# A hybrid attention and RWKV-7 layer in float32: later steps for transfers, norms and transposes handed on, one product tile for two heads

## The chip, the cores and the metric

The kernel runs on one core of a Trainium2 chip. The metric is the device time of one execution in microseconds; the median of several runs is given with the lowest and the highest.

## The reference

One encoder layer on x of 1024 positions by 1024 channels, all in float32. `proj` has 26 column tiles of 128: 12 for the attention's q, k and v, 14 for the recurrent part. The scan below runs forward and backward over all positions.

```python
h = _rms_norm(x, ln1_g)
proj = h @ w_in
q, k, v, u = proj[..., :512], proj[..., 512:1024], proj[..., 1024:1536], proj[..., 1536:]
attn = _dilated_window_attention(q, k, v, q_norm_g, k_norm_g)   # 8 heads of 64, 3 windows, ALiBi
rwkv = _rwkv7_bidirectional(u, ...)                             # 8 heads of 64
x = x + concatenate([attn, rwkv]) @ w_out
h = _rms_norm(x, ln2_g)
x = x + square(relu(h @ w_up)) @ w_down

def _dilated_window_attention(q, k, v, q_g, k_g):
    q = _rms_norm(q, q_g) * HEAD_DIM ** -0.5                    # norm over each head's 64 channels
    k = _rms_norm(k, k_g)
    ...
def step(state, inp):                                           # of _wkv7_scan
    r_t, w_t, k_t, v_t, kk_t, a_t = inp
    s_kk = einsum('bhvk,bhk->bhv', state, kk_t)
    state = state * w_t - s_kk * (kk_t * a_t) + v_t * k_t
    return state, einsum('bhvk,bhk->bhv', state, r_t)
```

## The kernel before

**Dense projections.** Each of the 26 column tiles is computed transposed (128 channels by 1024 positions) in two halves of 512 positions. Operands are split in a rounded and a remainder part, so one product is three matmuls (`mm3`, L105 to L107), and a half tile takes 8 × 3 = 24 of them. `proj` yields after every six. `dense()` runs the tiles in the order of a list: the recurrent tiles for head pair 0 first, then those for pairs 1, 2 and 3, then q, k and v tiles. At the end of each half tile `evac` takes the result out of PSUM. For q and k (`qk_tile`) it scales into `qc` (L322), squares it (`qsq`, L324), sums the squares by head on TensorE and inverts (`head_inv`, product L124, `rn` L127 and L128), widens that to 512 columns and takes the root (`rx`, L133), turns it on TensorE (L136), multiplies (`qc`, L326), splits into `qhi` and `qlo`, and stores both in DRAM (`qh_dr`/`kh_dr`, `ql_dr`/`kl_dr`, L332 and L333). For v it transposes and stores. `qsq`, `qhi` and the value tile `vn` share one buffer (tag `qt`).

**The recurrent part.** It is computed in chunks of 64 positions. For each head pair p (0 to 3) and each half of the positions, `per_half` computes the normed key, the transposed values (`VT`, stored to `vt_dr`, L432) and the decay (`om`, L443). `unit_a` then forms for each direction `al` and `bk`, their products for both heads (`psg`, L496, masked into `G`, L501), stores them to DRAM (`gd` and `rec_dr`), and turns `bk` (`psb`, L508, copied to `BK`, L512, stored by ScalarE's queue, L513). `bonus` is a small product. When both halves of a direction are ready, `pair_b` goes on the list `back`: it loads the diagonal 16 × 16 blocks as `MP` (L524), clears `Tt` (L527 and L528, POOL), inverts the blocks by a chain of 15 pairs of small VectorE instructions (`stmp`, L534, and L536), stores the result (`td`, L543) and loads it in another shape (`t16`, `t16t`, with `Ab`, L550 and L553). `unit_c` extends it to 64 × 64 by four products (`psd`, L564) and stores `TF`.

**What sets the order.** All these are Python generators, advanced by hand. `drive` runs one recurrent generator; after each yield it advances the first entry of `back` by 0.6 steps on average (`behind`) and the dense projections by 0.7 steps (`next(filler)`), a step being six matmuls or one `yield` between tiles. `until` runs projections until a tile that is needed is there. After the last head pair a loop empties `back`, four dense steps to each of its steps. The framework then schedules the instructions of each engine from this program order, and an instruction waits by semaphores for what it needs. DMAs are issued by SP, and a few by ScalarE (ACT) and POOL.

**After it.** `mixers` runs 16 steps of the scan (products `psc`, L870), two directions in each, with what is left of the projections and then the attention's pieces between them. Then come the output projection and the MLP.

## Time and profile before

| | |
|---|---|
| median of three runs | 1788.32 us (1781.92 to 1796.67) |
| the profiled execution | 1784.77 us |
| its span | 1783.0 us |
| mean granted TensorE clock | 0.949 |
| recurrent preparation, of the span | 151 to 510 us |
| the loop that empties `back` | 510 to 604 us |
| first scan steps with the last projections | 604 to 680 us |
| scan and attention | 680 to 990 us |
| output projection and MLP | 990 to 1783 us |

Engines are PE (TensorE), DVE (VectorE), ACT (ScalarE), POOL (GpSimd) and SP. PEld is TensorE's weight load. L12 is a line of the kernel before. A row of a timeline has start, duration, engine, line, operation, output<-inputs with their shapes, and in brackets the idle time before it with what ended it. A row of waits has the waiting engine and line, what it waited for, the total, the number of times and the longest. PEclk is the granted clock, as a share of full speed.

### The profile page before, as it was taken

Reading aid. Unit: us, or ns where it says so; the run is one execution under the profiler, and the core shown is the slowest. Engines: PE = TensorE matmul, PEld = TensorE weight load, DVE = VectorE, ACT = ScalarE, POOL = GpSimd, SP = SyncE. Lnnn points to the kernel's source line nnn. Section 1 sums busy time; section 2 is a strip of 40 time slices with the busy share of each in tenths; the row PEclk is TensorE's granted clock in tenths of the full one; section 3 lists DMA queues with packets and bytes.
Section 4 is the critical chain, followed back from the end, with each engine's and each line's share of the span. In section 5 each row is a group of like instructions: output and inputs, shape, how many; then the busy total and the mean of one; then the engine's idle time right before and its main releaser. Section 6 shows DMA issues by size and latency. Waiting matters only on the chain. (4 is left out here: it accounts for less than half of the span.)

```text
span 1783.0 us, 29922 instructions
## 1 busy us (share of the span) xinstructions
PE 1649.5 (93%) x11912; PEld 1365.7 (77%) x11912; DVE 861.9 (48%) x1754; ACT 543.5 (30%) x990; POOL 294.2 (16%) x322
## 2 busy tenths in 40 slices
PE   7999978979869997989998999999999999999999
PEld 6777767767757776877786887888888888888887
DVE  6655658757545424565775667332332233223321
ACT  5534334443412213535464234211121112112210
POOL 3022112222200000121223115200120012001200
PEclk9999989879879999988998999999999999999999
DMA  6155788878875599997973411111111111111121
GB/s 221 45 142 125 158 160 174 177 176 176 193 173 135 179 223 202 274 272 210 248 198 108 149 48 54 49 53 48 51 50 47 48 48 48 48 48 54 47 96 53
DMA packets 336923, 223.11 MB, mean 125 GB/s; under 512 B 238320, under 2 KB 289408, under 8 KB 332688
## 3 DMA queue, kind: packets, MB, share of 16 engines
q1 hardware_dynamic: 305520, 195.82, 42.7%
q10 hardware_dynamic: 27680, 15.38, 3.2%
q0 software_dynamic: 3584, 10.00, 2.5%
q8 instruction: 94, 1.54, 0.4%
q14 instruction: 45, 0.37, 0.1%
HBM read 150.22 MB, written 70.91 MB: 124 GB/s over the span
## 5 line engine op out<-in xcount | busy, mean ns | idle before, releaser
L101 ACT CAST w3h<-w3raw 128x512 fp32r<-128x512 f32 (+1 forms) x152 | 90.9, 600 | 397.0 <-PE ps L106 387.3
L106 PE MATMUL ps<-h2l,w3h 128*128 128x512 f32 x512 | 199.2, 389 | 1.1 <-DVE h2l L1045 1.1
L105 PE MATMUL ps<-h2h,w3h 128*128 128x512 f32 x512 | 199.3, 390 | 0.7 <-DVE x L1023 0.7
L107 PE MATMUL ps<-h2h,w3l 128*128 128x512 f32 x512 | 199.2, 389 | 0.0
L1089 POOL TENSOR_TENSOR relu<-relu 128x512 f32<-128x512 f32 x64 | 76.8, 1201 | 530.1 <-DVE relu L1088 530.1
L105 PE MATMUL ps_u<-hh,wh 128*128 128x512 f32 x368 | 156.1, 424 | 3.5 <-DVE ur L308 3.5
L107 PE MATMUL ps_u<-hh,wl 128*128 128x512 f32 x368 | 149.6, 407 | 0.0
L106 PE MATMUL ps_u<-hl,wh 128*128 128x512 f32 x368 | 149.3, 406 | 0.0
L102 DVE TENSOR_TENSOR w3l<-w3raw,w3h 128x512 fp32r<-128x512 f32 (+1 forms) x152 | 105.1, 693 | 79.7 <-ACT w3h L101 79.7
L1097 DVE TENSOR_TENSOR x<-x,ps 128x512 f32<-128x512 f32 x64 | 44.0, 688 | 181.7 <-PE ps L107 181.7
L105 PE MATMUL ps<-rw,w3h 128*128 128x512 f32 x320 | 124.7, 390 | 0.9 <-ACT w3h L101 0.9
L105 PE MATMUL ps<-f,w3h 128*128 128x512 f32 x320 | 124.7, 390 | 0.0
L106 PE MATMUL ps<-rw,w3h 128*128 128x512 f32 x320 | 124.5, 389 | 0.0
L107 PE MATMUL ps<-f,w3l 128*128 128x512 f32 x320 | 124.5, 389 | 0.0
L106 PE MATMUL ps<-f,w3h 128*128 128x512 f32 x320 | 124.5, 389 | 0.0
L107 PE MATMUL ps<-rw,w3l 128*128 128x512 f32 x320 | 124.1, 389 | 0.0
L106 PEld LDWEIGHTS ps<-h2l,w3h 128*128 128x128 f32 x512 | 96.1, 188 | 21.3 <-DVE h2l L1045 1.6
L105 PEld LDWEIGHTS ps<-h2h,w3h 128*128 128x128 f32 x512 | 96.1, 188 | 21.0 <-ACT w3h L101 1.1
L107 PEld LDWEIGHTS ps<-h2h,w3l 128*128 128x128 f32 x512 | 96.1, 188 | 19.9
L1088 DVE SCALAR_TENSOR_TENSOR relu<-ps,rep 128x512 f32<-128x512 f32 x64 | 44.1, 691 | 108.4 <-PE ps L107 108.2
L105 PEld LDWEIGHTS ps_u<-hh,wh 128*128 128x128 f32 x368 | 72.0, 196 | 20.2 <-DVE ur L308 4.3
L106 PEld LDWEIGHTS ps_u<-hl,wh 128*128 128x128 f32 x368 | 71.8, 195 | 16.7 <-issue 2.9
(331 smaller groups left out, 3228.7 us busy)
## 6 DMA issues: line engine op xcount, KB each, us to landing
rec<-rec_dr SPq DMA_DIRECT2D x32, 1152.0 KB, 10.0
w3raw<-in_w_up SPq DMA_DIRECT2D x64, 256.0 KB, 2.5
w3raw<-in_w_dn SPq DMA_DIRECT2D x64, 256.0 KB, 2.5
raw<-in_w_in SPq DMA_DIRECT2D x46, 256.0 KB, 2.9
rec_dr<-al POOLq DMA_DIRECT2D x64, 128.0 KB, 4.2
rec_dr<-G SPq DMA_DIRECT2D x32, 256.0 KB, 4.3
rec_dr<-G SPq DMA_DIRECT2D x64, 128.0 KB, 4.4
rec_dr<-BK ACTq DMA_DIRECT2D x16, 512.0 KB, 5.3
```

Of the source, the lines that this page charges most:

```text
L101: nc.scalar.copy(hi, raw)
L102: nc.vector.tensor_sub(lo, raw, r2f(hi))
L105: nc.tensor.matmul(ps, lh, rh, start=start, stop=False)
L106: nc.tensor.matmul(ps, lh, rl, start=False, stop=False)
L107: nc.tensor.matmul(ps, ll, rh, start=False, stop=stop)
L1088: nc.vector.scalar_tensor_tensor(t, pss[hf], 0.0, rep[:, HS[hf]], ALU.max, ALU.mult)
L1089: nc.gpsimd.tensor_mul(t, t, t)
L1097: nc.vector.tensor_add(x1[c][:, HS[hf]], x1[c][:, HS[hf]], ps)
```

## The change

- q, k and v tiles: `evac` now ends with the squares (for v with the scaled copy). What follows, `rest()`, goes on a list `late`. A new generator `later()` wraps `dense()` and advances the first entry of that list by one stage after each dense step: first the norm's product, inverse and widening, one step later the turn, the multiplication, the split and the stores. `qlo` now shares the buffer of `rx`.
- `per_half` yields twice more, after the squares and after the widening. `head_rep` is cut into `head_wide` and `head_turn` for this.
- `pair_b` yields three times instead of once between the load of `MP` and the chain, and three times (first half) or once (second half) between the loads of `Ab`, `t16`, `t16t` and the products.
- `bonus` yields ahead of its product rather than behind it.
- The products of both heads go to one tile of two banks, in a pool with one buffer; before, to two tiles of one bank in a pool with two.
- `behind` gets 0.8 instead of 0.6 per yield, the projections 0.62 instead of 0.7, and the loop that empties `back` runs two dense steps instead of four.

```diff
-    def head_rep(rn, sp, pp):
+    def head_wide(rn, sp):
         rx = sp.tile([P, 8, 64], F32, name="rx", tag="rx")
         nc.scalar.activation(rx, rn.rearrange("p (i o) -> p i o", o=1).to_broadcast([P, 8, 64]), AF.Sqrt)
+        return rx
+
+    def head_turn(rx, pp):
         psb = pp()
...
-            pg = s1.enter_context(tc.tile_pool(name="pg", bufs=2, side="right", space=PSUM, reuse_waits="tile"))
+            pg = s1.enter_context(tc.tile_pool(name="pg", bufs=1, side="right", space=PSUM, reuse_waits="tile"))
...
-                    rn = head_inv(sq, 1.0 / HD, NORM_EPS, tq, pq)
-                    nc.vector.scalar_tensor_tensor(qc, qc, qg8 if which == 0 else V("kg"), head_rep(rn, tq, pq), ALU.mult,
-                                                   ALU.mult)
-                    hi = tq.tile([P, 512], F32R, name="qhi", tag="qt")
-                    nc.scalar.copy(hi, qc)
-                    lo = tq.tile([P, 512], F32R, name="qlo")
-                    nc.vector.tensor_sub(lo, qc, r2f(hi))
-                    nc.sync.dma_start((qh_dr, kh_dr)[which][p][:, sl], r2f(hi))
-                    nc.sync.dma_start((ql_dr, kl_dr)[which][p][:, sl], r2f(lo))
+
+                    def rest():
+                        rn = head_inv(sq, 1.0 / HD, NORM_EPS, tq, pq)
+                        rx = head_wide(rn, tq)
+                        yield
+                        nc.vector.scalar_tensor_tensor(qc, qc, qg8 if which == 0 else V("kg"), head_turn(rx, pq), ALU.mult,
+                                                       ALU.mult)
+                        hi = tq.tile([P, 512], F32R, name="qhi", tag="qt")
+                        nc.scalar.copy(hi, qc)
+                        lo = tq.tile([P, 512], F32R, name="qlo", tag="rx")
+                        nc.vector.tensor_sub(lo, qc, r2f(hi))
+                        nc.sync.dma_start((qh_dr, kh_dr)[which][p][:, sl], r2f(hi))
+                        nc.sync.dma_start((ql_dr, kl_dr)[which][p][:, sl], r2f(lo))
+                        if hf == 1:
+                            T[4 * which + p - 12] = None
+                    late.append(rest())
                 yield from proj(4 * which + p, evac)
 
...
+                    def rest():
+                        ps = pq()
+                        for t in range(4):
+                            nc.tensor.transpose(ps[:, t * P:(t + 1) * P], vc[:, t * P:(t + 1) * P], ident)
+                        vn = tq.tile([P, 4, 2, 65], F32, name="vn", tag="qt")
+                        nc.gpsimd.memset(vn[:, :, :, 64:65], 1.0)
+                        nc.scalar.copy(vn[:, :, :, 0:64], ps.rearrange("p (t h e) -> p t h e", t=4, h=2))
+                        for h in range(2):
+                            nc.sync.dma_start(v_dr[p][h, sl].rearrange("(t p) f -> p t f", p=P), vn[:, :, h])
+                        if hf == 1:
+                            T[8 + p - 12] = None
+                        yield
+                    late.append(rest())
...
-                    T.setdefault(c - 12, None)
...
-            filler = dense()
+            late = []
+
+            def later():
+
+                for _ in dense():
+                    yield
+                    while late and next(late[0], 1) == 1:
+                        late.pop(0)
+                        break
+                while late:
+                    if next(late[0], 1) == 1:
+                        late.pop(0)
+                    yield
+            filler = later()
...
-                    behind(0.6)
+                    behind(0.8)
...
-                rn = head_inv(sq, 1.0, 1e-12, up, pp)
+                yield
+                rx = head_wide(head_inv(sq, 1.0, 1e-12, up, pp), up)
+                yield
                 kkn = w["kkn"] = up.tile([P, 512], F32, name="kkn")
-                nc.vector.scalar_tensor_tensor(kkn, kr[:, sl], V("kk", p), head_rep(rn, up, pp), ALU.mult, ALU.mult)
+                nc.vector.scalar_tensor_tensor(kkn, kr[:, sl], V("kk", p), head_turn(rx, pp), ALU.mult, ALU.mult)
...
-                    pss = [pg.tile([P, 4, P], F32, name="psg") for h in range(2)]
+                    pss = pg.tile([P, 2, 4, P], F32, name="psg")
                     for c in range(4):
                         for h in range(2):
-                            nc.tensor.matmul(pss[h][:, c], bk[H[h], 4 * g + c, h:h + 2].rearrange("p a b -> p (a b)"),
+                            nc.tensor.matmul(pss[:, h, c], bk[H[h], 4 * g + c, h:h + 2].rearrange("p a b -> p (a b)"),
                                              al[H[h], 4 * g + c].rearrange("p a b -> p (a b)"), start=True, stop=True)
...
-                        nc.vector.tensor_mul(Gs[h][:, 4 * g:4 * g + 4], pss[h], gm.to_broadcast([P, 4, P]))
+                        nc.vector.tensor_mul(Gs[h][:, 4 * g:4 * g + 4], pss[:, h], gm.to_broadcast([P, 4, P]))
...
-                pss = [pg.tile([P, 8, 64], F32, name="psb", tag="psg") for h in range(2)]
+                pss = pg.tile([P, 2, 8, 64], F32, name="psb", tag="psg")
...
                 for h in range(2):
-                    nc.scalar.copy(BK[:, :, h], pss[h])
+                    nc.scalar.copy(BK[:, :, h], pss[:, h])
                 nc.scalar.dma_start(rec_dr[d][:, cs, p, 256:384], BK.rearrange("p c h x -> p c (h x)"))
...
                 nc.gpsimd.memset(Tt.rearrange("p a b -> p (a b)")[:, 0:256:17], 1.0)
-                yield
+                for _ in range(3):
+                    yield
                 for s in range(1, 16):
...
+                    for _ in range(3 - 2 * hf):
+                        yield
                     yield from unit_c(dict(p=p, d=d, cs=slice(hf * 8, hf * 8 + 8), Ab=Ab, t16=t16, t16t=t16t))
...
+                yield
                 ps = pp()
                 nc.tensor.matmul(ps, K("blk"), bo, start=True, stop=True)
-                yield
                 nc.vector.tensor_mul(vr[:, sl], ps, vr[:, sl])
...
-                    drive(per_half(w), 0.7)
+                    drive(per_half(w), 0.62)
                     for d in range(2):
-                        gds[hf, d] = drive(unit_a(p * 4 + hf * 2 + d, w, d), 0.7)
+                        gds[hf, d] = drive(unit_a(p * 4 + hf * 2 + d, w, d), 0.62)
                         if hf == 1:
                             back.append(pair_b(p * 2 + d, p, d, [gds[z, d] for z in range(2)]))
                         if d == 1:
-                            drive(bonus(w), 0.7)
+                            drive(bonus(w), 0.62)
             while back:
                 behind(1.0)
-                for _ in range(4):
+                for _ in range(2):
                     next(filler, None)
```

The order of instructions on each engine moves as follows, at three places.

On PE, in the loop that empties `back`: `ps_u` are the dense matmuls, the two `psq` are the norm's product (from `qsq`) and the turn (from `rx`) of a q or k tile's half, `psd` are the products of `unit_c`. Before:

```order
L107 MATMUL ps_u<-hh_136,wl 128x512
L564 MATMUL psd<-t16t,Nb 64x64 x16
L124 MATMUL psq<-ct,qsq 128x2 x4
L564 MATMUL psd<-Yt,Nb 64x64 x16
L136 MATMUL psq<-ct,rx 128x128 x4
L105 MATMUL ps_u<-hh_129,wh 128x512
```

After:

```order
L124 MATMUL psq<-ct,qsq 128x2 x4
L598 MATMUL psd<-t_5712,Ab 64x64 x8
L139 MATMUL psq<-ct,rx 128x128 x4
L598 MATMUL psd<-t16t,Nb 64x64 x16
L598 MATMUL psd<-Yt,Nb 64x64 x16
L124 MATMUL psq<-ct,qsq 128x2 x4
L105 MATMUL ps_u<-hh_129,wh 128x512
```

Before, one half's norm and turn stand between two runs of 24 dense matmuls. Now the next half's norm follows the turn with two groups of products between them, and the dense matmuls of a whole tile come in one run.

On DVE, at the end of the last head pair's preparation: `bk` is made by the last `unit_a`, `us` by `bonus`, `qc` is a key tile's scaled half, and `stmp` is the first product of an inverse chain. Before:

```order
L481 SCALAR_TENSOR_TENSOR bk<-tm,Ei 128x8x64
L484 TENSOR_TENSOR bk<-kt,Ei 128x8x64
L591 TENSOR_TENSOR us<-pse,us 128x512
L534 TENSOR_TENSOR stmp<-Tt,MP 128x1
L536 TENSOR_REDUCE Tt<-stmp 128x1
L322 TENSOR_TENSOR qc<-ps_u,acc 128x512
```

After:

```order
L515 TENSOR_TENSOR bk<-kt,Ei 128x8x64
L326 TENSOR_TENSOR qc<-ps_u,acc 128x512
L102 TENSOR_TENSOR wl<-raw,wh 128x512
L604 TENSOR_TENSOR Nb<-psd,ct 128x512
L532 TENSOR_TENSOR G<-psg,ct 128x512 x2
L610 TENSOR_TENSOR Yt<-psd,t16t 128x512
L566 TENSOR_TENSOR stmp<-Tt,MP 128x1
L568 TENSOR_REDUCE Tt<-stmp 128x1
```

The chain's first product stood ahead of `qc`; now `qc` and five more instructions stand ahead of it.

On ACT, between head pair 0's last `unit_a` and head pair 1's first decay: `VT` and `om` are head pair 1's, `BK` is the turned `bk` of pair 0, and `th` is what `unit_a` begins with. Before:

```order
L432 DMA vt_dr<-VT 128x8x64
L512 COPY BK<-psb 128x8x64 x2
L513 DMA rec_dr_85<-BK 128x8x128
L443 ACT_TABLE_LOAD
L443 ACTIVATE om<-pse 128x512 x2
L617 CAST w0s<-wb 1x256
L456 ACTIVATE th<-pse,hv 128x512
```

After:

```order
L463 DMA vt_dr<-VT 128x8x64
L474 ACT_TABLE_LOAD
L474 ACTIVATE om<-pse 128x512 x2
L651 CAST w0s<-wb 1x256
L543 COPY BK<-psb 128x8x64 x2
L544 DMA rec_dr_85<-BK 128x8x128
L487 ACTIVATE th<-pse,hv 128x512
```

The copy and the store of `BK` moved from ahead of `om` to behind it; the store of `VT` stayed ahead of it.

More of the change, by code (lines that the diff above doesn't have):

```diff
@@ L200, in in_proj @@
                      [pa[0].tile([P, 512], F32, name="ps_u", tag="acc"), pd.tile([P, 512], F32, name="ps_u", tag="psd")],
-                     [pg.tile([P, 512], F32, name="ps_u", tag="psg") for _ in range(2)]]
+                     pg.tile([P, 2, 512], F32, name="ps_u", tag="psg")]
+            early[2] = [early[2][:, hf] for hf in range(2)]
             with tc.tile_pool(name="xp", bufs=2, side="right", reuse_waits="tile") as xp:
@@ L342, in evac @@
                     nc.vector.tensor_mul(vc, ps, rep[:, sl])
-                    ps = pq()
-                    for t in range(4):
-                        nc.tensor.transpose(ps[:, t * P:(t + 1) * P], vc[:, t * P:(t + 1) * P], ident)
-                    vn = tq.tile([P, 4, 2, 65], F32, name="vn", tag="qt")
-                    nc.gpsimd.memset(vn[:, :, :, 64:65], 1.0)
-                    nc.scalar.copy(vn[:, :, :, 0:64], ps.rearrange("p (t h e) -> p t h e", t=4, h=2))
-                    for h in range(2):
-                        nc.sync.dma_start(v_dr[p][h, sl].rearrange("(t p) f -> p t f", p=P), vn[:, :, h])
+                    def rest():
[11 more added lines that the diff above has]
+                    late.append(rest())
                 yield from proj(8 + p, evac)
@@ L904, in post @@
             rn = head_inv(ysq, 1.0 / HD, GN_EPS, rt, pbank)
-            ps = head_rep(rn, rt, pbank)
+            ps = head_turn(head_wide(rn, rt), pbank)
             for p in range(4):
```

2 lines of the change are left out of this document (1 added, 1 removed).

## The prediction

> **What bounds the kernel now.** I read the page's head first.
>
> ```profile
> PE 1649.5 (93%) x11912; PEld 1365.7 (77%) x11912; DVE 861.9 (48%) x1754; ACT 543.5 (30%) x990; POOL 294.2 (16%) x322
> PEclk9999989879879999988998999999999999999999
> DMA  6155788878875599997973411111111111111121
> ```
>
> TensorE (PE) is the bound: it idles only 1783.0 − 1649.5 = 133.5 us of the span. A change that removes no PE work can win that idle time, and the time in which the granted clock (PEclk) is below full. The busy times by stage come next: preparation of the recurrent heads (151 to 510), the back phase in which the last inverse chains run off (510 to 604), the scan's start with the rest of the dense projections (604 to 680), scan and attention (680 to 990), output projection and MLP. The columns are the window, its length, the busy us of PE, PEld, DVE, ACT and POOL, the granted clock, the share of the DMA engines and GB/s.
>
> ```profile
> 151.00:510.00 359.00, 305.33 (x3006) 252.96 (x3006) 232.39 (x498) 138.82 (x220) 85.43 (x135) 0.87 0.78 165
> 510.00:604.00 94.00, 80.50 (x871) 66.72 (x871) 46.22 (x101) 20.34 (x33) 1.60 (x6) 0.93 0.58 137
> 604.00:680.00 76.00, 67.33 (x674) 53.02 (x673) 21.60 (x45) 14.50 (x34) 0.69 (x6) 1.00 0.89 228
> 680.00:990.00 310.00, 273.20 (x3230) 234.77 (x3228) 188.21 (x577) 148.95 (x362) 67.56 (x37) 0.90 0.83 220
> 990.00:1783.00 793.00, 787.45 (x3490) 651.09 (x3488) 283.70 (x420) 150.74 (x248) 110.06 (x83) 1.00 0.17 55
> ```
>
> The last stage is PE from end to end and the change doesn't touch it; it gives the price of a dense matmul, 787.45 / 3490 = 0.2256 us. The idle time within reach is 359 − 305.33 = 53.7 us in the preparation and 94 − 80.50 = 13.5 us in the back phase, and a clock of 0.87 costs there up to 0.13 × 305 = 40 us more. Where it sits, the table of waits of 151 to 612 says (waiting engine and line, releaser; total, times, longest):
>
> ```profile
> PE psq L124 <- ACT qsq L324: 18.9, 10, 9.0
> PE pse L454 <- ACT om L443: 14.7, 3, 7.2
> DVE stmp L534 <- DMA MP<-gd: 28.2, 3, 10.7
> ```
>
> **The change part by part.** Each part is costed at the places where PE stands still.
>
> *A, the inverse chain before its load (head pair 3, 491 to 508).* DVE, PE, and the window that follows:
>
> ```profile
> 490.93 0.69 DVE L591 TENSOR_TENSOR us<-pse,us 128x512 f32<-128x512 f32 x1 [0.67 <-PE pse L589]
> 499.01 0.16 DVE L534 TENSOR_TENSOR stmp<-Tt,MP 128x1 f32<-128x1 f32 x1 [7.39 <-DMA MP<-gd]
> 499.28 0.68 DVE L322 TENSOR_TENSOR qc<-ps_u,acc 128x512 f32<-128x512 f32 x1
> 500.67 1.86 PE L124 MATMUL psq<-ct,qsq 128*128 128x2 f32 x8 [4.88 <-ACT qsq L324]
> 498.00:508.00 10.00, 7.33 (x62) 6.59 (x62) 8.37 (x32) 1.26 (x2) 0.00 (x0) 0.51 0.48 135
> ```
>
> DVE stands 7.39 us at the chain's first product; the key tile's `qc` is queued behind it, so PE gets its squares 4.88 us late and then runs at 0.51: 4.88 + 7.33 × 0.49 = 8.5 us. With three yields instead of one, `qc` and six more DVE instructions stand ahead of that product (the order of the change shows them). They are of the 0.6 us kind, about 4 us, and SP issues the first of the pair's loads ahead of the `td` stores and the second right behind them, both ahead of the `t` loads that they followed before. `qc` waits for nothing there. A gains 8. DVE may still wait 3 us at the chain; behind it then stands nothing that PE needs at once.
>
> *B, the same pair's first direction (422 to 433).*
>
> ```profile
> 422.76 0.16 DVE L534 TENSOR_TENSOR stmp<-Tt,MP 128x1 f32<-128x1 f32 x1 [4.62 <-POOL Tt L528]
> 426.88 0.44 PE L564 MATMUL psd<-t,Ab 64*64 64x64 f32 x2 [4.23 <-DVE bk L484]
> 427.00:433.00 6.00, 6.00 (x56) 5.48 (x56) 4.43 (x11) 2.30 (x4) 4.78 (x9) 0.50 1.00 247
> ```
>
> DVE waits for POOL's memset and PE idles 4.23 us, then runs at half clock: 4.23 + 6.00 × 0.50 = 7.2. After the change 46 dense matmuls stand between the value transposes and the decay product there, 13 before: 33 × 0.2256 = 7.4 us of cover. B gains 7.
>
> *C, ACT's own DMA issues (255 to 263, and 356 to 364 alike).*
>
> ```profile
> 262.32 0.79 PE L454 MATMUL pse<-xa,wh 128*128 128x512 f32 x1 [6.64 <-ACT om L443]
> 257.74 0.37 ACTq L432 DMA_DIRECT2D vt_dr<-VT  x1
> 258.20 1.07 ACT L512 COPY BK<-psb 128x512 f32<-128x512 f32 x2 [5.76 <-DMA t<-td]
> 259.98 0.37 ACTq L513 DMA_DIRECT2D rec_dr<-BK  x1
> 260.38 1.28 ACT L443 ACT_TABLE_LOAD   x1 [1.10 <-DMA gd<-G]
> ```
>
> ACT can't issue `vt_dr` or `rec_dr` until an older transfer of SP's has landed; `om` stands behind both, and PE behind `om`. The change puts the copy and store of `BK` behind `om`, and leaves `vt_dr` ahead of it. So the 5.76 us can stay and only what follows it can go. Two such waits make up 6.64 + 7.2 of the 14.7 us. Bounds: nothing (the wait sits at `vt_dr` in both) and 14.7 + 2 × 3 (half clock, as in B) = 20. I take one case in two, 10.
>
> *D, the first key tile of the back phase (518 to 536).*
>
> ```profile
> 527.27 0.63 ACT L324 ACTIVATE qsq<-qc 128x512 f32<-128x512 f32 x1 [9.01 <-DMA kh_dr<-qhi]
> 527.96 1.86 PE L124 MATMUL psq<-ct,qsq 128*128 128x2 f32 x8 [9.04 <-ACT qsq L324]
> 522.00:536.00 14.00, 8.04 (x53) 7.19 (x54) 5.13 (x23) 1.88 (x3) 1.60 (x6) 0.51 0.92 209
> ```
>
> One buffer (tag `qt`) serves the squares, the high half and the value tile; the squares wait until the store of the high half has landed. PE loses 9.04 + 8.04 × 0.49 = 13 us. Here norm and squares now stand a dense step apart, and the queue's rush of loads has passed earlier: D gains 13, with nothing as the other bound.
>
> *E, the earlier MP load.* Of the 28.2 us of DVE waits, 28.2 − 7.39 = 20.8 are two others, with no PE wait of that size behind them. The change also puts one later load behind stores of `td`. Between −6 and +3; I take −2.
>
> *F, what the back phase loses.* Before, each half tile has 24 dense matmuls ahead of the next norm. After, by its order, a tile's two halves follow each other with only two of the inverse chain's products (`psd`) between them, four times. The buffer's cycle in a quiet stretch:
>
> ```profile
> 555.02 0.17 DVE L127 TENSOR_SCALAR rn<-psq 128x8 f32<-128x8 f32 x1 [0.66 <-PE psq L124]
> 555.46 0.63 ACT L133 ACTIVATE rx<-rn 128x512 f32<-128x512 f32 x1 [1.58 <-DVE rn L128]
> 556.14 0.65 PE L136 MATMUL psq<-ct,rx 128*128 128x128 f32 x4
> 556.91 0.75 DVE L326 SCALAR_TENSOR_TENSOR qc<-qc,qg,psq 128x512 f32<-128x512 f32 x1
> 557.69 0.62 ACT L329 CAST qhi<-qc 128x512 fp32r<-128x512 f32 x1 [1.60 <-DVE qc L326]
> 558.34 0.33 SPq L332 DMA_DIRECT2D qh_dr<-qhi  x1
> kl_dr<-qlo SPq DMA_DIRECT2D x3, 256.0 KB, 3.8
> 563.10 0.63 ACT L324 ACTIVATE qsq<-qc 128x512 f32<-128x512 f32 x1 [4.79 <-DVE qc L322]
> 562.21 1.15 PE L564 MATMUL psd<-Yt,Nb 64*64 64x64 f32 x32
> 569.78 0.57 SPq L332 DMA_DIRECT2D kh_dr<-qhi  x1
> ```
>
> From the turn's end at 556.79 to the store's issue at 558.34 are 1.55 us, then the landing, 3.8 us for such a transfer, then 0.63 for the squares: 6.0 us, and 1.5 more where the issue stands behind loads of the chain, as the one at 569.78 does. The cover is two products, 2 × 1.1 = 2.2 us. PE waits between 3.8 and 5.3 us; a transfer that lands at the scan's quickest could take a microsecond off. I take 4.0, four times: 16. The turn itself comes 1.1 us after the norm's product (555.02 to 555.46 + 0.63 = 556.09) and has half a product, 0.55, as cover: four times 0.5, 2 in all. Then the clock. In 321 to 330:
>
> ```profile
> 323.50 0.33 PE L564 MATMUL psd<-t,Ab 64*64 64x64 f32 x2 [2.19 <-DMA t<-td]
> 326.00:330.00 4.00, 4.00 (x40) 3.66 (x40) 2.99 (x9) 0.00 (x0) 1.01 (x1) 0.50 0.36 100
> ```
>
> A gap of 2.19 us, among short products, was already followed by half clock, as those of 4.23, 4.88 and 9.04 were; the 0.42 us gaps of the back phase were not. So between two and four of the places cost about 3 us more each (B's 3.0): 6 to 12, and I take 9. F costs 16 + 2 + 9 = 27. The Trainium skill ("TensorE: Matmul & The Clock Gate", section "HAM oscillation — how this bites in real kernels") puts the limit at an idle gap of about 3.4 us. By that page alone a gap of 2.19 would keep its clock, which this trace contradicts; and shorter places among the four would cost nothing, so F would be near its lower bound.
>
> *G, the dense matmuls that move.* By the order, 131 dense matmuls more stand ahead of the first scan product, and 96 of them ahead of the last chain product: the stages up to 604 grow by 96 × 0.2256 = 21.7 us of PE work. The scan's start has that much less to do. It gives back all 21.7 if PE set its length (67.33 us busy of 76), and as little as (1 − 0.89) × 76 = 8.4 if the transfers did. PE's share is the nearer: I take 20, G costs 2, at most 13.3.
>
> The larger shared product tile has the same matmuls and masks; one buffer of two banks replaces two of one bank, so a direction's next group waits for both masks. PE waited there before too (0 to 3 us, held in the range). The turned bonus yield moves nothing PE waits for.
>
> Sum: −8 − 7 − 10 − 13 − 2 + 27 + 2 = −11, on the profiled execution's 1784.77 us (1783.0 and 1.8 around): 1774 us. That execution lies 0.2% under the median of 1788.32.
>
> **The rivals.**
>
> *R1, slower: the back phase becomes a chain through one buffer.* F at its slow end: four places at 5.3 + 0.5 + 3.6 = 9.4 us, 38; G at its slow end, 13; C and E give nothing, A, B and D their 28. That is +23: 1808 us. It decides where the store lands later than 3.8 us after its issue. For it: kh_dr waited 9.01 us in D. Against it: the DMA share of this stage is the lowest of the four ahead of the tail, 0.58. The same clock page describes such a loop, in which every round pays for its own gap; the trace of before has it nowhere in a row.
>
> *R2, no change: the waits move to the same transfers.* With the DMA engines at 0.78 to 0.89, a load that is asked for earlier lands no earlier, and the transfers ahead of `om` still hold ACT. A, C and E give nothing; B, D, F and G stay: −7 − 13 + 27 + 2 = +9, 1794 us. For it: 5.76 of C's wait sits at a store that stays. Against it: A's gain comes from `qc` standing ahead, not from the landing. The Trainium skill ("DMA: Bandwidth & Descriptors", section "Issuing engines are not separate DMA queues") says the same of transfers issued from different engines: they share 16 engines and interleave.
>
> *R3, larger gain: the back phase is covered.* The halves come further apart at run time than the static order has them, F costs only 3, all of C's 20 goes, G at 2: −50 + 3 + 2 = −45, 1740 us. For it: PE is kept in order by semaphores alone and ACT and SP have room in the back phase (20.34 us busy of 94). Against it: the buffer count of `qt` is one.
>
> **How the numbers follow.** The forecast gets 0.42, R3 0.25, R1 0.25, R2 0.08. The forecast's own range is 1758 to 1790: E, G and F's gaps at their bounds, 10 to 16 us either way. This kernel's runs spread so that about 1% is the least that can be told from no change: 1766.9 and 1802.6 on the profiled time. Below it lie R3 and three tenths of the forecast, 0.25 + 0.13 = 0.38; above it R1, 0.25; the rest, 0.37, is within. The range goes from 1735 to 1812: the lower two fifths of R3 and the upper two fifths of R1 are left out, 0.2.
>
> **What would show it.** A: the wait of `stmp` for MP remains, but no PE gap of over 2 us near the last pair's end. B: no gap of 4 us at 422. C: `om` waits total about 7 us and their releaser is a copy of `VT`'s store. D and F: in the back phase no 9 us gap, but four of about 4 us at the norm's product, with granted clock near 0.5 behind them, and a stage that is longer by 20 to 40 us. G: the scan's start, from the first scan product on, is shorter by about 20 us. The prediction is wrong if the back phase shows no gaps at the norms (R3), if the scan's start keeps its length, or if new gaps come at the shared product tile.

## The result and the profile after

| | before | changed |
|---|---|---|
| median of the runs on one chip | 1785.49 us (1781.92 to 1796.67, 4 runs) | 1832.36 us (1830.14 to 1836.49, 4 runs) |
| ratio | | 1.0254, 95% interval 1.0203 to 1.0306 |
| span of the profiled execution | 1783.0 us | 1829.7 us |

The forecast was 1774 us in a range of 1735 to 1812. The change is slower by 46.7 us in the two profiles. The page's head of the changed kernel:

```profile
PE 1647.0 (90%) x11912; PEld 1367.2 (75%) x11912; DVE 861.3 (47%) x1754; ACT 548.7 (30%) x994; POOL 293.4 (16%) x322
PEclk9998987988887896798898899999999999999999
```

TensorE is busy for 2.5 us less than before. Its idle time went from 133.5 to 1829.7 − 1647.0 = 182.7 us, and these 49 us are the loss. To see where, the span is cut at events that both kernels have: the first bonus product, the last `psg` product, the last `psd`, the first and the last `psc` of the scan, and the first sum of the MLP's norm. The stages are the preparation, the last loop, what lies ahead of the scan, the scan, and what is left of the attention with the output projection. Before, and then after, with window, length and the busy times as in the prediction:

```profile
140.50:506.40 365.90, 312.45 (x3016) 258.85 (x3012) 233.76 (x497) 143.64 (x227) 85.56 (x137) 0.87 0.78 168
506.40:602.90 96.50, 83.19 (x906) 68.61 (x904) 48.95 (x109) 19.92 (x33) 1.60 (x6) 0.92 0.57 135
602.90:611.70 8.80, 7.17 (x38) 5.78 (x36) 3.19 (x6) 2.39 (x5) 0.00 (x0) 1.00 0.81 252
611.70:942.50 330.80, 296.26 (x3627) 250.46 (x3626) 180.53 (x538) 139.08 (x344) 56.08 (x36) 0.93 0.90 232
942.50:1090.00 147.50, 135.98 (x678) 112.36 (x677) 98.27 (x179) 56.46 (x109) 45.45 (x27) 0.94 0.30 97
```

```profile
135.70:526.00 390.30, 312.22 (x3092) 255.45 (x3090) 240.85 (x488) 146.44 (x231) 82.92 (x137) 0.87 0.76 159
526.00:656.00 130.00, 113.72 (x974) 94.37 (x973) 57.44 (x134) 25.25 (x41) 0.66 (x4) 0.84 0.46 114
656.00:670.50 14.50, 14.50 (x69) 11.72 (x69) 2.08 (x3) 1.17 (x2) 1.49 (x7) 1.00 0.83 208
670.50:975.20 304.70, 251.70 (x3389) 217.15 (x3389) 159.85 (x493) 125.80 (x312) 54.49 (x29) 0.85 0.93 238
975.20:1136.80 161.60, 144.21 (x756) 121.32 (x756) 104.32 (x210) 67.62 (x133) 47.51 (x28) 0.93 0.30 97
```

Length minus PE busy is TensorE's idle time. It grew in the preparation from 53.5 to 78.1 us (+24.6), in the last loop from 13.3 to 16.3 (+3.0), in the scan from 34.5 to 53.0 (+18.5) and behind it from 11.5 to 17.4 (+5.9). The last loop is 33.5 us longer mostly because it holds more work: PE is busy 113.72 us there against 83.19, with 265 dense matmuls in its record against 192, and the granted clock is 0.84 there against 0.92.

The table of waits of the changed kernel from 151 to 670 us, TensorE's and then VectorE's rows (waiting engine and line, releaser; total, times, longest). The third and the fourth answer to `qsq` and `om` of the prediction, the last two to `MP`:

```profile
PE psd L598 <- DVE Yt L610: 24.0, 7, 9.6
PE psg L527 <- DVE G L532: 16.0, 5, 7.5
PE psq L124 <- ACT qsq L328: 10.5, 8, 2.3
PE pse L485 <- ACT om L474: 6.5, 2, 5.5
DVE G L532 <- DMA rec_dr<-G: 27.2, 6, 10.9
DVE stmp L566 <- DMA MP<-gd: 12.6, 4, 5.3
DVE stmp L566 <- POOL Tt L559: 18.5, 2, 10.7
```

Two of the waits that the change aimed at are smaller: `qsq` 10.5 us instead of 18.9 with none above 2.3, and `om` 6.5 instead of 14.7. The third is not. `MP` fell from 28.2 to 12.6 us, but the same instruction, the chain's first product, now waits 18.5 us until POOL has cleared `Tt`, so it stands 31.1 us in all, against 28.2 + 4.6 = 32.8 before. TensorE waits for `Yt` and `G` instead, 40.0 us in all. Three rows of before, from 151 to 612 us, to compare:

```profile
PE psd L564 <- DVE Yt L576: 4.3, 4, 1.7
PE psg L496 <- DVE G L501: 9.0, 7, 4.0
DVE stmp L534 <- POOL Tt L528: 4.6, 1, 4.6
```

One such place, on DVE and PE of the changed kernel:

```profile
252.15 0.69 DVE L532 TENSOR_TENSOR G<-psg,ct 128x512 f32<-128x512 f32 x1 [10.87 <-DMA rec_dr<-G]
252.76 0.68 DVE L610 TENSOR_TENSOR Yt<-psd,t16t 128x512 f32<-128x512 f32 x1
253.50 0.80 PE L598 MATMUL psd<-Yt,Nb 64*64 64x64 f32 x10 [9.46 <-DVE Yt L610]
```

`G` can't be written until the store of its buffer's last content has landed. DVE stands there for 10.87 us, `Yt` is queued behind, and TensorE has nothing else to do. Before, the wait at this place was 2.48 us long:

```profile
247.93 0.69 DVE L501 TENSOR_TENSOR G<-psg,ct 128x512 f32<-128x512 f32 x1 [2.48 <-DMA rec_dr<-G]
```

Not every wait at `Yt` is one for `G`. The longest, of 9.60 us at 283.92, has another chain behind it: ScalarE stood for a load (`wb`), and VectorE stood for ScalarE ahead of `Yt`:

```profile
279.26 0.40 ACT L652 CAST wbh<-wb 1x256 fp32r<-1x256 f32 x1 [6.10 <-DMA wb<-in_w2w]
281.98 1.28 DVE L316 SCALAR_TENSOR_TENSOR us<-ur,vt,us 128x1024 f32<-128x1024 f32 x1 [8.10 <-ACT us L315]
```

In the scan two waits are longer. One is TensorE's own for the first steps' loads. In the other it waits for ScalarE's copy `pts` of the attention, and at the longest of these ScalarE had stood for a load. The rows of the changed kernel, and one of before:

```profile
PE psc L904 <- DMA pv<-vt_dr: 22.1, 4, 11.5
704.54 1.11 PE L904 MATMUL psc<-pv,rec 128*64 128x64 f32 x15 [11.46 <-DMA pv<-vt_dr]
PE pv L761 <- ACT pts L756: 9.3, 3, 6.1
752.78 0.24 ACT L722 CAST qh<-qh 128x64 fp32r<-128x64 f32 x1 [6.78 <-DMA vB<-v_dr]
PE psc L870 <- DMA pv<-vt_dr: 11.5, 4, 5.6
```

Before, the wait for `pts` was 0.9 us. Together the two grew by 19.0 us. The changed kernel has 13 dense matmuls left when the scan begins, the kernel before has 144.

### The profile page after: what moved, and what is told of

Same layout as the page of the kernel before. It is cut to its first block, busy times and chain, and to the rows that moved or that the text cites. A ratio compares the mean times of both kernels' runs of the same rounds, so it can differ in the third digit from the quotient of the medians.

```text
span 1829.7 us, 29944 instructions
## 1 busy us (share of the span) xinstructions
PE 1647.0 (90%) x11912; PEld 1367.2 (75%) x11912; DVE 861.3 (47%) x1754; ACT 548.7 (30%) x994; POOL 293.4 (16%) x322
## 5 line engine op out<-in xcount | busy, mean ns | idle before, releaser
L106 PE MATMUL ps_u<-hl,wh 128*128 128x512 f32 x368 | 154.1, 419 | 0.0
L107 PE MATMUL ps_u<-hh,wl 128*128 128x512 f32 x368 | 154.1, 419 | 0.0
L107 PEld LDWEIGHTS ps_u<-hh,wl 128*128 128x128 f32 x368 | 74.7, 203 | 17.1 <-issue 0.7
```

The source lines that it names most:

```text
L106: nc.tensor.matmul(ps, lh, rl, start=False, stop=False)
L107: nc.tensor.matmul(ps, ll, rh, start=False, stop=stop)
```

## The experiments

Four theories were to be told apart. S: SP's queue holds the stores of `G` behind stores of the inverse chain, and VectorE and TensorE wait behind them. T: the shared tile makes the products of the two heads wait for each other. H: what is handed on holds SP's queue and the single buffer. G, after the forecast's term: too few dense matmuls are left to cover the loads of the scan's start. All ratios are to runs of the kernel before on the same chip.

**The tile.** First the changed kernel with two tiles again:

```diff
-            pg = s1.enter_context(tc.tile_pool(name="pg", bufs=1, side="right", space=PSUM, reuse_waits="tile"))
+            pg = s1.enter_context(tc.tile_pool(name="pg", bufs=2, side="right", space=PSUM, reuse_waits="tile"))
...
-                    pss = pg.tile([P, 2, 4, P], F32, name="psg")
+                    pss = [pg.tile([P, 4, P], F32, name="psg") for h in range(2)]
```

> The changed kernel (1832 us), with only the product tile put back: two tiles of one bank, two buffers. Theory S (SP's queue: stores of the head products stand behind inverse-chain stores that wait, so VectorE waits at G for its old buffer and TensorE behind it): the tile is not the cause, 1825 to 1835 us, and the 7 to 9.5 us gaps of TensorE in the preparation remain. Theory T (one buffer for both heads makes each next product wait for both masks): TensorE's waits at psg for G, 16.0 us in the changed kernel against 9.0 before, go back by 7 or more with their half clock, 1810 to 1820 us. Theory H (the norms and transposes handed on hold SP's queue and the single buffer): 1825 to 1835 us.

Measured: 1808.99 us, ratio 1.0143 (1.0122 to 1.0165), 1 us below T's window and 16 below those of S and H. Then the tile alone, as the only difference from the kernel before (the same diff read the other way):

> The kernel before with one part of the change alone: the shared product tile of two banks in a pool with one buffer. 120 dense matmuls stay behind the scan's first product (144 before, 13 in the changed kernel). Theory T (the shared tile makes TensorE and VectorE wait for each other and for G's stores in the preparation): TensorE's idle time in the preparation, 53.5 us before and 78.1 in the changed kernel, goes to 70 or more; 1800 to 1810 us. If the tile costs only in company with the other parts: 1780 to 1790 us.

Measured: 1807.72 us, ratio 1.0107 (1.0074 to 1.0141), in T's window. The preparation's rows, of the tile alone and of the changed kernel without it:

```profile
137.00:528.70 391.70, 317.65 (x3122) 260.55 (x3120) 240.68 (x487) 146.94 (x231) 81.68 (x137) 0.86 0.76 159
```

```profile
136.70:504.70 368.00, 316.16 (x2973) 261.64 (x2969) 233.41 (x493) 142.92 (x227) 83.68 (x137) 0.87 0.78 166
```

With the tile TensorE idles 391.7 − 317.65 = 74.0 us in the preparation, without it 368.0 − 316.16 = 51.8. So the tile costs some 20 us, in company (1.0254 − 1.0143 = 0.011) or alone (0.0107). The prediction had it at 0 to 3.

How it costs them was tried in two ways. One takes away a reason for the wait at `G`, with a third buffer:

```diff
-                Gs = [up.tile([P, 8, P], F32, name="G", bufs=2) for h in range(2)]
+                Gs = [up.tile([P, 8, P], F32, name="G", bufs=3) for h in range(2)]
...
-                    g2t = up.tile([P, P], F32, name="g2t")
+                    g2t = up.tile([P, P], F32, name="g2t", tag="stmp")
```

> The changed kernel with three buffers for G instead of two (a 0.5 KB weight tile shares another tile's buffer to make room). Nothing is left for the scan, as in the changed kernel. If VectorE's waits at G for the old buffer's store (27.2 us in 6) are what stops TensorE in the preparation, TensorE's idle time there goes from 78 us to 60 or less and the time to 1808 to 1820 us. If the shared product tile itself is (TensorE waits for both masks, whatever G waits for), it stays above 70 and the time at 1827 to 1837 us.

Measured: 1837.46 us, ratio 1.0258 (1.0222 to 1.0293), half a microsecond above the second window. The other takes the chain's stores out of SP's queue, where the changed kernel had them ahead of G's:

```diff
-                        nc.sync.dma_start(diag(td), src[H[hf]])
+                        nc.gpsimd.dma_start(diag(td), src[H[hf]])
```

> The changed kernel with the stores of the inverse chains (td) issued by POOL instead of SP; the numbers of dense matmuls in each stage stay within two of the changed kernel's. In the changed kernel SP holds the stores of G behind the td stores it put ahead of them, and VectorE waits at G. If that order of SP's queue is how the shared product tile costs its time (theory S through T): VectorE's 27.2 us at G fall below 15, TensorE's idle time in the preparation from 78 us to 63 or less, 1812 to 1822 us. If the two heads' coupling through the tile itself costs it: 75 or more, 1827 to 1840 us. A cost of POOL's own, its issues being busy time there, could add up to 10.

Measured: 1833.16 us, ratio 1.0280 (1.0253 to 1.0306), in the second window. VectorE's waits at `G`, of the first and of the second:

```profile
DVE G L532 <- DMA rec_dr<-G: 15.5, 3, 8.8
```

```profile
DVE G L532 <- DMA rec_dr<-G: 26.3, 7, 11.2
```

The third buffer took the waits at `G` from 27.2 to 15.5 us, and TensorE's idle time in the preparation stayed at 78.0. Without the `td` stores on SP the waits stayed (26.3 us), and the idle time at 75.0. So theory S fell: it isn't the order of SP's queue, and the wait at `G` isn't the whole of it. What a trace shows besides is that the tile changes where the dense matmuls stand. Before, 19 of them stand between the turn of `bk` (237.27) and the chain's next product (242.48); in the kernel with the tile alone none do, and TensorE comes to the stores' wait earlier and empty. Its wait there with the tile alone:

```profile
253.22 1.98 PE L595 MATMUL psd<-Yt,Nb 64*64 64x64 f32 x32 [9.61 <-DVE Yt L607]
```

Whether the joint wait for both heads costs time itself (T), or only through this other order, was not separated: no run has the new tile with the old order of the dense matmuls. So the tile's price is shown, and how it comes about is not.

**The dense matmuls left for the scan.** Undoing two other parts gave back as much as the tile. The chain's yields:

```diff
-                for _ in range(3):
-                    yield
+                yield
                 for s in range(1, 16):
...
-                    for _ in range(3 - 2 * hf):
-                        yield
```

> The changed kernel without the added yields of the inverse chain (one again after the MP load, none between the t loads and the products). Theory S: the chain ends earlier relative to the next unit's stores, the td stores wait less ahead of them, 1805 to 1820 us. Theories T and H: 1827 to 1840 us, with MP waits of VectorE back above 20 us.

Measured: 1805.11 us, ratio 1.0117 (1.0087 to 1.0148). And the handing on:

```diff
-                    late.append(rest())
+                    for _ in rest():
+                        pass
```

> The changed kernel with the second part of each q, k and v half tile run at once, as before (nothing handed on; qlo in its own buffer). Theory H: SP's wait at the q and k stores (46.9 us against 28.9 before) and the gaps at the norms in the last loop go, 1805 to 1815 us. Theories S, T and G: 1825 to 1840 us; the first key tile of the last loop then has its 9 us gap again.

Measured: 1807.00 us, ratio 1.0120 (1.0088 to 1.0151). The first lies in S's window, though S had no support in the trace above, and the second in H's. In both the preparation idles as in the changed kernel (78.4 and 74.3 us). What they share is something that no part names: 128 and 120 dense matmuls are left when the scan begins, instead of 13, and TensorE idles 27.5 and 31.4 us in the scan instead of 53.0. That can be had with no part undone, by one dense step fewer in the last loop:

```diff
-                for _ in range(2):
+                for _ in range(1):
                     next(filler, None)
```

> The changed kernel with one dense step instead of two per step of the loop that empties the list of inverse chains; all else as changed. 121 dense matmuls then stay behind the scan's first product. Theory G (the scan's start has nothing left that covers its loads): TensorE's idle time in the scan goes from 53 us to about 33, the gap of 11.5 us at the third scan step goes, 1808 to 1816 us. If the three parts that were undone one by one each had its own cost, and the dense matmuls left for the scan are only a by-product: 1827 to 1840 us.

Measured: 1818.54 us, ratio 1.0167 (1.0140 to 1.0194), which is 0.0087 or 15.5 us less than the changed kernel; the expectation's window was missed by 2.5 us. Its scan's row, and its wait for the first steps' loads:

```profile
632.90:929.50 296.60, 263.30 (x3372) 223.56 (x3371) 153.62 (x468) 118.32 (x287) 45.70 (x30) 0.88 0.95 240
PE psc L904 <- DMA pv<-vt_dr: 8.7, 3, 4.6
```

TensorE idles 296.6 − 263.3 = 33.3 us there, and the wait for these loads fell from 22.1 to 8.7 us. The other way round, the paces of before empty the store altogether:

```diff
-                    behind(0.8)
+                    behind(0.6)
...
-                for _ in range(2):
+                for _ in range(4):
                     next(filler, None)
```

(with 0.7 for 0.62 at the three `drive` calls)

> The changed kernel with the paces of before: inverse chain 0.6, dense 0.7, four dense steps per step of the last loop. About 131 dense matmuls go back behind the start of the scan. Theory S (the chain's faster pace brings its waiting stores ahead of the products' stores): 1800 to 1815 us, most of it in the preparation. A fourth theory G, that the dense matmuls taken from the scan's start leave it waiting for transfers (gap of 11.5 us at the third scan step, PE idle in scan and attention 53 + 16 us against 35 + 10): 1812 to 1820 us, with the gain in scan and attention. Theories T and H: 1827 to 1837 us.

Measured: 1841.41 us, ratio 1.0326 (1.0305 to 1.0348): slower than the changed kernel, where every theory had expected faster or the same. The assumption in it that dense matmuls go back behind the scan's start was wrong: none is left, all 1248 are done before it. The chain's yields alone, on the kernel before, use up the store as well:

```diff
-                yield
+                for _ in range(3):
+                    yield
                 for s in range(1, 16):
...
+                    for _ in range(3 - 2 * hf):
+                        yield
```

> The kernel before with one part alone: three yields after the MP load, three or one after the loads of Ab and t. No dense matmul stays behind the scan's first product (144 before). Theory G: idle time of TensorE in the scan and just ahead of it goes from 36 us to 50 to 60 and the preparation, without the shared tile, stays at 50 to 58: 1800 to 1815 us. If the yields cost nothing and the dense matmuls left over are only a by-product: 1780 to 1792 us.

Measured: 1803.78 us, ratio 1.0107 (1.0069 to 1.0144). Its preparation, what lies between the last loop and the scan, and the scan:

```profile
141.10:498.40 357.30, 325.37 (x2795) 268.15 (x2793) 231.65 (x482) 144.25 (x230) 83.23 (x137) 0.89 0.79 171
643.70:664.10 20.40, 0.01 (x2) 0.03 (x1) 0.69 (x1) 0.79 (x3) 0.00 (x0) 0.54 0.99 258
664.10:965.20 301.10, 263.29 (x3483) 227.66 (x3485) 173.63 (x534) 133.96 (x334) 63.15 (x32) 0.90 0.90 232
```

For 20.4 us hardly an engine does anything but wait: the DMA engines are at 0.99 with loads of the attention, which SP issued first, and of the scan's first step. The yields also bring the preparation's idle time to 31.9 us. There is less of the chain in it: 1186 of the chain's products lie in the preparation instead of 1440, and the last loop is 145.3 us long instead of 96.5. Over the whole span the two nearly cancel: TensorE idles 1793.6 − 1663.4 = 130.2 us, 3 less than before. The span of the profiled run, the fastest of four, is 10.6 us longer because TensorE is busy for 13.9 us more. So this run shows where the idle time of an uncovered scan stands, but not that it sets the time.

Over these kernels the two effects on the idle time stand apart. The idle times are length minus PE busy of the rows by stage; the last column is TensorE's busy time in the whole span, for the same 11912 matmuls:

| kernel | ratio | idle in the preparation | dense left for the scan | idle ahead of and in the scan | TensorE busy |
|---|---|---|---|---|---|
| shared tile: changed | 1.0254 | 78.1 | 13 | 53.0 | 1647.0 |
| ... td stores by POOL | 1.0280 | 75.0 | 13 | 51.5 | 1652.6 |
| ... three G buffers | 1.0258 | 78.0 | 0 | 59.2 | 1664.7 |
| ... paces of before | 1.0326 | 68.8 | 0 | 61.3 | 1655.4 |
| ... one dense step in the loop | 1.0167 | 75.8 | 121 | 35.3 | 1652.7 |
| ... chain's yields out | 1.0117 | 78.4 | 128 | 27.5 | 1647.3 |
| ... nothing handed on | 1.0120 | 74.3 | 120 | 35.0 | 1650.3 |
| ... tile alone | 1.0107 | 74.0 | 120 | 38.2 | 1648.7 |
| two tiles: before | 1 | 53.5 | 144 | 36.2 | 1649.5 |
| ... chain's yields alone | 1.0107 | 31.9 | 0 | 58.2 | 1663.4 |
| ... handing on alone | 1.0185 | 51.7 | 112 | 38.2 | 1681.5 |
| ... changed without the tile | 1.0143 | 51.8 | 118 | 36.5 | 1661.4 |

With the shared tile the preparation idles 69 to 78 us, without it 32 to 54. With 13 or fewer dense matmuls left TensorE idles 51 to 61 us ahead of and in the scan, with 112 or more 28 to 38. The idle time is not the whole price: the busy time differs by up to 35 us. Undoing the tile, for one, took 38 us of idle time from the changed kernel's span and added 14 us of busy time.

**The handing on.** As the only difference from the kernel before (for v tiles alike, with `later()` as the dense generator):

```diff
-                    rn = head_inv(sq, 1.0 / HD, NORM_EPS, tq, pq)
+                    def rest():
+                        rn = head_inv(sq, 1.0 / HD, NORM_EPS, tq, pq)
+                        rx = head_wide(rn, tq)
+                        yield
...
+                    late.append(rest())
```

> The kernel before with one part of the change alone: the second part of each q, k and v half tile one dense step later, qlo in the buffer of rx. 112 dense matmuls stay behind the scan's first product. By the forecast's terms D and F: the 9 us gap at the first key tile of the last loop goes (-13) and four gaps of about 4 us at the norms come (+27): 1795 to 1805 us. If the halves come apart at run time as the changed kernel's gaps of 1.8 to 2.3 us say, F is 4 x 2 and its clock, about 10 to 14: 1780 to 1788 us. Theory H (this part holds SP's queue and delays all behind it): above 1805 us.

Measured: 1822.28 us, ratio 1.0185 (1.0156 to 1.0214), above all windows but the last. The forecast doesn't describe it. It is in H's window, but the delay that H names is not seen: the preparation idles as before, the last loop 19.5 us instead of 13.3. Waits at the norm in that loop are there, the longest of the size that F had, all four together 10.6 us where F had 16:

```profile
PE psq L124 <- ACT qsq L327: 10.6, 4, 4.0
```

But the whole span has 1817.1 − 1681.5 = 135.6 us of idle time, 2 more than before, and TensorE is busy for 32 us more with the same matmuls:

```profile
PE 1681.5 (93%) x11912; PEld 1392.9 (77%) x11912; DVE 861.2 (47%) x1754; ACT 551.1 (30%) x996; POOL 293.6 (16%) x322
508.80:631.90 123.10, 103.65 (x993) 85.19 (x992) 54.70 (x117) 25.05 (x40) 1.60 (x6) 0.87 0.46 117
642.30:978.90 336.60, 300.04 (x3564) 253.82 (x3564) 175.36 (x520) 137.59 (x335) 54.52 (x34) 0.86 0.86 222
```

The granted clock is 0.87 in the last loop (0.92 before) and 0.86 in the scan (0.93). Over the span it is 0.931 against 0.949. An estimate from these two: 0.069 × 1817.1 − 0.051 × 1783.0 = 34 us more of full clock are missing, about the 32 us by which TensorE is busy longer. To see whether the one buffer of the tag `qt` is the reason, it was given two, and the last loop one dense step, so that the scan keeps more of them (172):

```diff
-                    sq = tq.tile([P, 512], F32, name="qsq", tag="qt")
+                    sq = tq.tile([P, 512], F32, name="qsq", tag="qt", bufs=2)
...
-                for _ in range(4):
+                for _ in range(1):
                     next(filler, None)
```

(`qhi` and `vn` alike)

> The kernel before with the handing on alone, but with two buffers instead of one for the squares, the high halves and the value tiles (tag qt), and one dense step per step of the last loop so that the scan keeps dense matmuls (172 behind its first product). If the single buffer is what the handing on costs (term F: the squares wait for the store of the high half): TensorE's waits at the norms in the last loop fall below 4 us in all and the time from 1822 to 1775 to 1790 us. If the cost lies elsewhere, in the slower clock behind other gaps: 1800 us or more.

Measured: 1798.09 us, ratio 1.0078 (1.0044 to 1.0111), between the two windows. The norm's waits are gone from the last loop. TensorE idles 1799.5 − 1676.4 = 123.1 us, less than before, and is still busy for 27 us more. Two things were changed here, so how much of the gain against 1822 us is the buffer's is not separated:

```profile
PE 1676.4 (93%) x11912; PEld 1391.2 (77%) x11912; DVE 859.0 (48%) x1754; ACT 543.3 (30%) x990; POOL 291.6 (16%) x322
```

The same two buffers in the changed kernel without the tile and without the chain's yields:

```diff
-                    hi = tq.tile([P, 512], F32R, name="qhi", tag="qt")
+                    hi = tq.tile([P, 512], F32R, name="qhi", tag="qt", bufs=2)
```

> The changed kernel with two product tiles again and without the inverse chain's added yields, so with the handing on, the paces and the preparation's yields; and two buffers for the tag qt. 76 dense matmuls stay behind the scan's first product. Against the same without handing on (1770 us, one buffer): if the handing on is good once it has its buffer, 1755 to 1770 us; if it costs whatever buffer it has, 1785 us or more.

Measured: 1802.12 us, ratio 1.0099 (1.0065 to 1.0133): it costs whatever buffer it has. Against the same kernel with nothing handed on and one buffer, which comes next, its span is 40.9 us longer: 12.7 us of that is idle time and 28.2 busy time, at a mean granted clock of 0.936 against 0.952. So without the tile the longer part of the price is matmuls at a lower clock, and the single buffer can only be in the rest. In the changed kernel itself the handing on shows as idle time: undone, it gives back 26 us of it and 3 us more of busy time come. Why the clock stays lower in the scan (0.86 and 0.87 in the two kernels with the handing on alone, 0.93 before), when norms are handed on far ahead of it, is open.

**What is left.** With the tile, the chain's yields and the handing on undone, the paces, the shorter last loop, and the added yields of the preparation's first part and of `bonus` remain of the change (against the kernel before):

```diff
-                    behind(0.6)
+                    behind(0.8)
...
-                    drive(per_half(w), 0.7)
+                    drive(per_half(w), 0.62)
...
-                for _ in range(4):
+                for _ in range(2):
                     next(filler, None)
```

> What is left of the change when the shared tile, the inverse chain's yields and the handing on are all undone: paces of 0.8 and 0.62, two dense steps per step of the last loop, the added yields of the preparation's first part and of the bonus. 142 dense matmuls stay behind the scan's first product, as before (144). If the three undone parts are the whole loss: idle time of TensorE in the preparation 50 to 58 us, in the scan 30 to 37, 1778 to 1792 us. If the paces have a cost of their own: above 1797 us.

Measured: 1769.79 us, ratio 0.9925 (0.9897 to 0.9953), 8 us below its window and faster than both kernels. Its preparation and last loop:

```profile
140.60:507.80 367.20, 318.92 (x3050) 265.76 (x3048) 236.62 (x493) 151.17 (x237) 83.98 (x137) 0.90 0.79 170
507.80:587.10 79.30, 69.30 (x841) 56.76 (x840) 45.11 (x112) 16.06 (x26) 1.60 (x6) 0.94 0.63 145
```

TensorE idles 48.3 and 10.0 us (53.5 and 13.3 before) at 0.90 and 0.94 of full clock (0.87 and 0.92), and 142 dense matmuls are left for the scan. Putting the chain's yields back into it:

```diff
-                yield
+                for _ in range(3):
+                    yield
                 for s in range(1, 16):
...
+                    for _ in range(3 - 2 * hf):
+                        yield
```

> The changed kernel with two parts undone: two product tiles again, and the second part of each q, k and v half tile run at once. The inverse chain's yields, the paces and the preparation's yields stay. 168 dense matmuls stay behind the scan's first product. The yields of the chain alone took TensorE's idle time in the preparation from 53.5 us to 31.9 and lost it again ahead of a scan with nothing left to cover its loads. If these two effects are separate (theory G), the preparation idles 30 to 42 us here and the scan 28 to 37, with no gap ahead of it: 1750 to 1768 us, less than both kernels. If the gain of the yields was only time moved into the last loop: 1765 to 1780 us, as with the yields undone (1770).

Measured: 1780.52 us (12 runs), ratio 0.9968 (0.9948 to 0.9987), half a microsecond above the second window. The preparation idles 50.1 us, not 30 to 42, and the last loop is 91.9 us long against 79.3 without the yields. So the yields gain nothing here though 168 dense matmuls are left for the scan: the shorter idle time that they had alone did not come back.

## Why the prediction was wrong

- **The larger tile.** "PE waited there before too (0 to 3 us, held in the range)" is the step that failed first. It measured about 20 us, and the prediction's own sign of being wrong, new gaps at the shared product tile, came: TensorE's waits at `psg` for `G` went from 9.0 to 16.0 us. One buffer of two banks was taken as the same memory with another grain; that the grain decides where other work stands was not looked at. Whether the order or the joint wait is what costs stays open.
- **G.** The second step that failed. The moved work was right, though the sum priced only the 96 that move ahead of the last chain product: 131 × 0.2256 = 29.6 us ahead of the scan's first product. From there to the MLP's norm before took 330.8 + 147.5 = 478.3 us and now takes 304.7 + 161.6 = 466.3. It gave back 12.0 of the 29.6, so G cost 17.6, where 2 was taken and 13.3 was the bound. The bound came from the DMA share of a window whose PE work covered the loads; without that work the waits at `psc` doubled, from 11.5 to 22.1 us. One dense step fewer in the last loop gave 15.5 us back.
- **A, B and C.** The gaps named went or shrank, and the gain didn't come. In the changed kernel the norm's product of A and the `psd` of B stand 0 and 0.2 us, and `om` (C) lost one of its two long waits, 14.7 to 6.5 us. But near A's place TensorE stands 5.06 us at `psg` for `G`, and 7.54 us at the `psg` at 478.43, where 1.4 and 4.0 us were before. Without the tile it is little better: the four gaps of A, B and C, 22.9 us before, are 6.9 us there, and still the preparation idles 51.8 us against 53.5, at the same clock of 0.87, where 25 us were forecast to go. The time came back at other products: there TensorE waits 10.0 us for `t` and 9.7 us for `Yt` in the preparation, 2.2 and 3.6 us before. "Behind it then stands nothing that PE needs at once" was wrong in the changed kernel: `G`'s wait stood there. (The order shows five more DVE instructions ahead of the chain's product, not six, and B's chain is head pair 2's; neither changes the sum.)
- **E.** The `MP` waits fell, as told above, only by changing their name: the chain's first product stands 31.1 us instead of 32.8, since POOL's clearing of `Tt` had to wait for the store of its last content. An earlier load gained nothing that can be seen.

```profile
215.72 0.31 POOL L558 MEMSET Tt<- 128x256 f32 x1 [7.50 <-DMA td<-Tt]
```

- **D** went as forecast: no wait at the norm's product above 2.3 us. Nothing handed on, chain's yields kept and two tiles, it is back at 9.3 us.
- **F.** Four gaps of over 1 us came at the norms, of 1.87, 1.75, 2.31 and 1.25 us, 7.2 in all where 16 was taken; the last loop's clock fell from 0.92 to 0.84. Without the tile, or with the handing on alone, one gap each had the size forecast, 4.1 and 4.0 us. Its clock term was too small in kind: it counted 3 us behind each gap of the last loop, and the handing on alone cost 33 us (1.0185) with only 2 us more idle time than before.
- **The rivals.** R1 had the right sign and a price, 1808, that was still too low; its mechanism isn't what happened, since the last loop idles only 3.0 us more. R2's price, 1794, is out, but its mechanism is in part what the preparation shows: the wait at the chain's first product stayed, for another transfer, and other waits came at the stores of `G`. R3 is out: the gaps at the norms came.

The three parts don't add up: undone one by one they gave back 20, 24 and 24 us (0.0111, 0.0137 and 0.0134 of 1785), together 59 (0.0329) and not 68. Each of them alone already restored the scan's cover (118 to 128 dense matmuls left), which can be gained only once; that this is the whole difference is not shown.

From the timeline of the changed kernel, two of F's gaps and the one at `psg` for `G`:

```profile
544.54 1.05 PE L124 MATMUL psq<-ct,qsq 128*128 128x2 f32 x8 [1.87 <-ACT qsq L328]
607.79 1.87 PE L124 MATMUL psq<-ct,qsq 128*128 128x2 f32 x8 [2.31 <-ACT qsq L328]
478.43 1.86 PE L527 MATMUL psg<-al,bk 64*128 64x128 f32 x14 [7.54 <-DVE G L532]
```

## What to carry to other kernels

Work that can go anywhere is a store that covers later transfers: before a change that spends it earlier is priced, count what is left of it for the next stage that starts on loads. A buffer that is shared more widely is not the same memory with another shape, since it changes what must be done together and so where everything else stands. Of a change in several parts, the parts are worth measuring one by one: here undoing any one of three gave back 20 to 24 us, and with all three undone what remained gained 0.75%.

## What was not expected of the hardware

The lower clock outlasts the idle time that it follows. In the kernel with two buffers and the handing on, in the attention behind the scan:

```profile
930.00:939.90 9.90, 7.03 (x61) 6.45 (x61) 7.31 (x21) 7.12 (x15) 3.19 (x2) 1.00 0.11 29
945.00:955.00 10.00, 9.96 (x46) 9.31 (x45) 3.52 (x14) 4.10 (x10) 0.00 (x0) 0.50 0.23 74
955.00:965.00 10.00, 10.00 (x48) 9.64 (x47) 4.11 (x22) 5.46 (x15) 0.00 (x0) 0.50 0.81 278
965.00:975.00 10.00, 9.96 (x47) 8.95 (x47) 5.23 (x16) 2.60 (x8) 9.38 (x5) 0.50 0.60 245
```

For 30 us TensorE is busy nearly all the time, and the granted clock is 0.50. Up to 939.9 us it was 1.00, and the longest idle time of TensorE from 930 to 945 us was 1.60 us. The prediction's price of about 3 us behind a gap can't hold for such a stretch. The Trainium skill ("TensorE: Matmul & The Clock Gate", section "HAM oscillation — how this bites in real kernels") names idle gaps above about 3.4 us as what lowers the clock; this trace has it lowered behind shorter ones.
